# Order of ScalarE's work between attention and the GLU in a hybrid S5/attention block: the gates' sigmoids behind the last attention copies and v's second rounded half

## The chip, the cores and the metric

One core of a Trainium2 chip runs the whole block in one launch. The metric is the device time of an execution in microseconds (us); the kernel before takes 375.18 us, the median of three runs (375.08, 375.18 and 377.10).

## The reference

The block is a decoder layer over 256 tokens of width 1024. What matters here is its first half:

```
u = rms_norm(h, g_pre_mix)
z = u @ w_in                                  # [ssm | q | k | v | gate_A | gate_B]
y_a = v * sigmoid(v @ w_glu + b_glu)          # v = gelu(S5 output)
y_b = softmax(causal(q @ k.T / 8)) @ v_att    # 8 heads of 64
merged = sigmoid(z_ga) * (y_a @ w_branch_a) + sigmoid(z_gb) * (y_b @ w_branch_b)
h = h + rms_norm(merged @ w_out, g_post_mix)
f = square(relu(rms_norm(h, g_pre_ffn) @ w_ff1)) @ w_ff2
h = h + rms_norm(f, g_post_ffn)
```

All matrices are float32. With 256 tokens there is a single attention block, so the attention is causal over all of them.

## The kernel before, in words

**Weights in pieces.** The weights stream from HBM as pieces of 128x1024 float32 (512 KB), numbered in the order of use: 0 to 31 are `w_in` (ssm, k, q, v, then four chunks of gates, four pieces each; 28 to 31 are the last gates chunk), 32 and 33 `w_glu`, 34 to 37 `w_branch_b`, 38 to 41 `w_branch_a`, 42 to 49 `w_out`, then the MLP. SyncE's queue starts the loads, three raw buffers deep. Each piece is cut in two rounded parts: ScalarE (ACT in the profile) copies it to `w_hi` (L180), VectorE (DVE) subtracts to get `w_lo` (L181). Activations are cut in the same way (`v_h`, `v_l`; `yb_h`, `yb_l`; `ya_h`, `ya_l`). A product is then three matmuls, hi by hi, hi by lo and lo by hi (`three`, L204 to L206), and one piece is 24 matmuls of 256 columns (2 blocks of K, 4 of output, 3 products). There are five `w_hi`/`w_lo` buffers; `w_hi` of piece j waits until TensorE (PE) is done with piece j-5.

**Two K blocks per piece.** The GLU product v @ w_glu needs K blocks 0 and 1 with piece 32 and blocks 2 and 3 with piece 33; v's blocks 0 and 1 come from the first half of the S5 outputs (`outputs(0, v)`), blocks 2 and 3 from the second (`outputs(1, v)`, L1003). The first w_branch_b product likewise needs attention's first head group with piece 34 and the second group with piece 35.

**Attention.** For each of two head groups: scores (L1027), masked maximum (DVE, L1034), exp (ACT, L1041), normalising (DVE, L1048), transposes on PE (L1058, L1059 into two tiles; L1064 into a third), their copies to SBUF on ACT (`pT0`, two copies, L1060; `pT1`, L1065), then the products with the values (L1076) and the copy and subtraction to `yb_h` (ACT, L1079) and `yb_l` (DVE, L1080).

**ACT's function tables.** Exp, gelu and sigmoid each need a table load on ACT (ACT_TABLE_LOAD rows); plain copies (`AF.Copy`) run between them without one. A helper keeps functions of one table together by telling the scheduler what an instruction must come behind:

```
def table(name, inst, *before):
    for b in before:
        if b in last_act:
            follow(inst, last_act[b])
    last_act[name] = inst
```

`follow(later, earlier)` adds an order without a semaphore: a scheduler fixes the order of instructions on each engine when the program is built, from priorities and these orders, and on the chip each engine takes its instructions in that order. `sigmoid` (L437) serves the gates (`gate`: gate B in `sg_87`, gate A in `sg_86`, four sigmoids of 128x512 each) and the GLU (`sgl`, four of 128x256).

**Order around the change.** After the second gelu ACT has, in this order: a table load, seven gate sigmoids, the two `pT0` copies of the second group, `v_h`'s second half, the `pT1` copy, `w_hi` of piece 36, the eighth gate sigmoid, `w_hi` of piece 37, `yb_h`, and the GLU's sigmoids with `w_hi` of piece 38 among them. PE has the first half of the GLU, then the value products (L1076) with the GLU's second half around them, then w_branch_b.

Of the kernel before, what the change touches and what calls it, by code (L numbers as in the profile page):

```python
# [13 lines left out]
AF = mybir.ActivationFunctionType  # L14
# [4 lines left out]
P = 128  # L19
# [52 lines left out]
def pair_b(t):  # L72
    return t.unsqueeze(1).to_broadcast([P, 2, T])
# [3 lines left out]
def tile_hybrid_block(ctx, tc, a, out):  # L77


    nc = tc.nc  # L80
# [30 lines left out]
    def follow(later, earlier):  # L111

        tc.add_manual_dep(later.ins, earlier.ins.name, ORDER, reason="order")

    last_act, hold, marks, mains = {}, {}, {}, {}
# [7 lines that stand above are left out]
# [56 lines left out]
    def split(hi, lo, src):  # L179
        i = nc.scalar.activation(hi, src, AF.Copy)  # L180
        j = nc.vector.tensor_tensor(lo, src, hi.bitcast(F32), op=ALU.subtract)  # L181
        return i, j
# [174 lines left out]
    att = Attention(nc, att_pool, mask, ident, aux, table, soon)  # L357
# [68 lines left out]
    for g in range(2):  # L426
        for c in range(2):
            ps = chunk(KT, xh, xl)
            for j in range(2):
                s = sg[g][:, 4 * c + 2 * j:4 * c + 2 * j + 2, :]  # L430
                nc.vector.tensor_tensor(s, ps[j], pair_b(rs_b), op=ALU.mult)
    follow(s5.first_state[1], mains[28, 1])
    s5_pool.close()
    yb_h, yb_l = att.yb_h, att.yb_l

    def sigmoid(o, i, **kw):
        table("sigmoid", nc.scalar.activation(o, i, AF.Sigmoid, **kw), "gelu")  # L437

    def gate(g, c):
        for j in range(2):  # L440
            s = sg[g][:, 4 * c + 2 * j:4 * c + 2 * j + 2, :]
            sigmoid(s, s)
# [5 lines left out]
    v_h = mid.tile([P, 4, T], F32R, name="v_h")  # L448
    v_l = mid.tile([P, 4, T], F32R, name="v_l")
# [9 lines left out]
    vf = v.rearrange("p m b a -> p m (b a)")  # L459
    for j in range(2):  # L460
        js = slice(2 * j, 2 * j + 2)
        split(v_h[:, js, :], v_l[:, js, :], vf[:, js, :])

    def branch_b(c):
        pb = chunk(4, yb_h, yb_l)
# [5 lines left out]
    with ahead():  # L471
        for h in range(2):
            sgl = mid.tile([P, 2, T], F32, name="sgl", bufs=2)
            hs = slice(2 * h, 2 * h + 2)
            for e in range(2):
                sigmoid(sgl[:, e, :], ps[h][:, e, :], bias=b_glu[:, 2 * h + e:2 * h + e + 1])
            nc.vector.tensor_tensor(sgl, sgl, vf[:, hs, :], op=ALU.mult)
            for e in range(2):
                m = 2 * h + e
                split(ya_h[:, m, :].rearrange("p (a b) -> p b a", b=L), ya_l[:, m, :].rearrange("p (a b) -> p b a", b=L),  # L480
                      sgl[:, e, :].rearrange("p (b a) -> p b a", b=L))
# [69 lines left out]
    def turn(tt, kts, get=aux):  # L551

        tp = get((P, len(kts), P))
        for e, kt in enumerate(kts):
            i = nc.tensor.transpose(tp[:, e, :], h_tok[:, tt, P * kt:P * kt + P], ident)
        return tp, i
# [40 lines left out]
    for kts in (lower, upper):  # L597
        tp, _ = turn(1, kts)
# [6 lines left out]
    with at(SECOND):  # L605
        for tt in range(2):
            ss = small.tile([P, 2], F32, name="ss")
            for c in range(2):
                junk = small.tile([P, 512], F32, name="junk")
                i = nc.scalar.activation(junk, h_tok[:, tt, 512 * c:512 * c + 512], AF.Square, scale=1.0 / 32,  # L610
                                         accum_out=ss[:, c:c + 1])
# [73 lines left out]
class S5:  # L685
# [228 lines left out]
    def transposes(self):  # L914

        nc, B4 = self.nc, self.B4
        self.B4T = B4T = [t.rearrange("p i b c -> p i (b c)") for t in B4]
        for i4 in range(4):
            for j in range(2):
                tp = self.aux((P, 4, P))  # L920
                with self.soon() as side:
                    for i in range(4):
                        side(nc.tensor.transpose(tp[:, i, :], B4T[j][:, 4 * i4 + i, :], self.ident))
                nc.scalar.activation(B4T[j][:, 4 * i4:4 * i4 + 4, :], tp, AF.Copy)  # L924
# [81 lines left out]
class Attention:  # L1006
# [43 lines left out]
    def transposes(self):  # L1050

        nc, (p0, p1) = self.nc, self.prob
        for f in range(2):
            tp = self.aux((P, 2, T))
            with self.soon() as side:
                for e in range(2):
                    h = 2 * f + e
                    side(nc.tensor.transpose(tp[:, e, 0:P], p0[:, h, :], self.ident))  # L1058
                    side(nc.tensor.transpose(tp[:, e, P:T], p1[:, h, 0:P], self.ident))  # L1059
            nc.scalar.activation(self.pT0[:, 2 * f:2 * f + 2, :], tp, AF.Copy)  # L1060
        tp = self.aux((P, 4, P))
        with self.soon() as side:
            for h in range(4):
                side(nc.tensor.transpose(tp[:, h, :], p1[:, h, P:T], self.ident))  # L1064
        nc.scalar.activation(self.pT1, tp, AF.Copy)  # L1065

    def values(self, g, v_tok):
        nc = self.nc
# [88 lines left out]
```

## Time and profile before

| | us |
|---|---|
| median of 3 runs | 375.18 |
| the profiled execution, its own time | 375.54 |
| its span, first to last instruction | 373.7 |
| time outside the span (375.54 - 373.7) | 1.84 |
| PE busy in the span | 358.7 |
| DVE busy | 267.2 |
| ACT busy | 212.7 |

Times in the views below count from the start of the span. PE, DVE, ACT, POOL and SP are TensorE, VectorE, ScalarE, GpSimd and SyncE; L437 is line 437 of the kernel before. A row of the timeline gives start and duration, and in brackets the idle time before it with what ended that idle time. PEclk is the granted TensorE clock: 1.00 is 2.4 GHz and 0.50 is 1.2 GHz. Matmuls are pipelined, so their rows overlap and the distance between two starts is what one costs.

### The profile page before, as it was taken

What the parts mean: (1) busy time and instruction counts of PE and PEld (TensorE: products, weight loads), DVE (VectorE), ACT (ScalarE), POOL (GpSimd) and SP (SyncE); (2) the same over time, 40 slices, a digit from 0 to 9 for tenths busy, and PEclk for the clock granted to TensorE, in tenths of its full rate; (3) what the DMA queues carried; (4) which work ended last, traced back from release to release, by engine and by line L of the source; (5) the groups of instructions that cost most, each with busy time, mean ns of one, the idle gap of its engine ahead of it and who ended that gap; (6) DMA issues with size and microseconds to landing.
All of it is one profiled execution on the core that took longest, in us unless ns stands there. A gap on an engine that the chain in (4) does not pass through costs nothing.

```text
span 373.7 us, 7568 instructions
## 1 busy us (share of the span) xinstructions
PE 358.7 (96%) x3073; PEld 324.6 (87%) x3073; DVE 267.2 (71%) x459; ACT 212.7 (57%) x322; POOL 36.6 (10%) x46
## 2 busy tenths in 40 slices
PE   7999999999999869999999999999999999999993
PEld 6999979997998659998878989899898989989882
DVE  4999899999679826796768584655656475565633
ACT  4894539997963896454548653535345353533511
POOL 4005300001000000000001030202002020100200
PEclk9999999999999988999999999999999999999999
DMA  7966845465061525655634646665566656555303
GB/s 207 348 199 187 234 165 179 154 200 175 31 220 61 188 97 164 182 188 186 228 123 158 217 151 217 210 219 189 190 194 190 194 185 201 192 193 191 127 0 113
DMA packets 19604, 65.84 MB, mean 176 GB/s; under 512 B 2640, under 2 KB 3280, under 8 KB 19440
## 3 DMA queue, kind: packets, MB, share of 16 engines
q1 hardware_dynamic: 18624, 64.66, 53.4%
q0 software_dynamic: 512, 0.53, 0.6%
q8 instruction: 24, 0.39, 0.4%
q10 hardware_dynamic: 432, 0.17, 0.2%
q14 instruction: 12, 0.10, 0.1%
HBM read 63.77 MB, written 1.05 MB: 173 GB/s over the span
## 4 chain that ended last, share of the span: by engine, by line
PE 60%; ACT 12%; DVE 11%; DMA 10%; issue 4%; POOL 1%; SPq 0%; DVEq 0%; POOLq 0%; ACTq 0%
PE acc L211 10%; PE acc L210 10%; PE acc L209 10%; DMA w_raw<-in_w_in_dram 9%; PE aux L204 8%; PE aux L206 8%; PE aux L205 8%; DVE w_lo L181 4%; ACT w_hi L180 3%; ACT Tl L951 2%; PE acc L204 1%; PE acc L205 1%; PE acc L206 1%; DMA w_raw<-in_w_glu_dram 1%; ACT B L924 1%
## 5 line engine op out<-in xcount | busy, mean ns | idle before, releaser
L180 ACT ACTIVATE w_hi<-w_raw 128x1024 fp32r<-128x1024 f32 (+2 forms) x119 | 121.3, 1025 | 123.7 <-PE aux L205 37.4
L181 DVE TENSOR_TENSOR w_lo<-w_raw,w_hi 128x1024 fp32r<-128x1024 f32 (+2 forms) x119 | 139.7, 1177 | 70.7 <-ACT w_hi L180 70.3
L204 PE MATMUL acc<-xh,w_hi 128*128 128x256 f32 x224 | 63.2, 287 | 1.5 <-ACT w_hi L180 1.5
L205 PE MATMUL acc<-xl,w_hi 128*128 128x256 f32 x224 | 63.3, 286 | 0.0
L204 PE MATMUL aux<-h_h,w_hi 128*128 128x256 f32 x224 | 62.2, 278 | 0.0
L205 PE MATMUL aux<-h_l,w_hi 128*128 128x256 f32 x224 | 61.9, 276 | 0.0
L206 PE MATMUL aux<-h_h,w_lo 128*128 128x256 f32 x224 | 61.8, 276 | 0.0
L206 PE MATMUL acc<-xh,w_lo 128*128 128x256 f32 x224 | 60.5, 286 | 0.0
L210 PE MATMUL acc<-w_lo,f_h 128*128 128x512 f32 x128 | 50.0, 392 | 0.0
L211 PE MATMUL acc<-w_hi,f_l 128*128 128x512 f32 x128 | 49.9, 394 | 0.0
L209 PE MATMUL acc<-w_hi,f_h 128*128 128x512 f32 x128 | 49.5, 388 | 0.0
L204 PEld LDWEIGHTS acc<-xh,w_hi 128*128 128x128 f32 x224 | 43.1, 193 | 2.8 <-ACT w_hi L180 2.4
L205 PEld LDWEIGHTS acc<-xl,w_hi 128*128 128x128 f32 x224 | 43.4, 194 | 0.8 <-issue 0.7
L204 PEld LDWEIGHTS aux<-h_h,w_hi 128*128 128x128 f32 x224 | 42.1, 188 | 0.3
L205 PEld LDWEIGHTS aux<-h_l,w_hi 128*128 128x128 f32 x224 | 42.1, 188 | 0.3
L206 PEld LDWEIGHTS acc<-xh,w_lo 128*128 128x128 f32 x224 | 41.5, 192 | 0.9 <-issue 0.5
L206 PEld LDWEIGHTS aux<-h_h,w_lo 128*128 128x128 f32 x224 | 42.0, 188 | 0.0
L69 POOL TENSOR_TENSOR r<-r 128x512 f32<-128x512 f32 x14 | 17.8, 1289 | 128.7 <-ACT f_h L647 128.7
L210 PEld LDWEIGHTS acc<-w_lo,f_h 128*128 128x128 f32 x128 | 24.0, 188 | 5.3
L209 PEld LDWEIGHTS acc<-w_hi,f_h 128*128 128x128 f32 x128 | 24.0, 188 | 5.1
L211 PEld LDWEIGHTS acc<-w_hi,f_l 128*128 128x128 f32 x128 | 24.1, 188 | 4.8
L649 DVE TENSOR_TENSOR f_l<-r,f_h 128x512 fp32r<-128x512 f32 x14 | 15.3, 1095 | 6.5 <-POOL r L69 6.5
(245 smaller groups left out, 564.6 us busy)
## 6 DMA issues: line engine op xcount, KB each, us to landing
w_raw<-in_w_ff_dram SPq DMA_DIRECT2D x64, 512.0 KB, 4.8
w_raw<-in_w_in_dram SPq DMA_DIRECT2D x31, 512.0 KB, 4.2
w_raw<-in_w_out_dram SPq DMA_DIRECT2D x8, 512.0 KB, 4.7
w_raw<-in_w_bb_dram SPq DMA_DIRECT2D x4, 512.0 KB, 4.8
w_raw<-in_w_ba_dram SPq DMA_DIRECT2D x4, 512.0 KB, 4.0
w_raw<-in_w_glu_dram SPq DMA_DIRECT2D x2, 512.0 KB, 4.4
x_tok<-in_xt_dram SPq DMA_DIRECT2D x1, 1024.0 KB, 8.0
g_row<-in_rows_dram SPq DMA_DIRECT2D x2, 512.0 KB, 6.1
```

What stands on the lines that cost most here:

```text
L69: return nc.gpsimd.tensor_tensor(o, x, y, op=op)
L180: i = nc.scalar.activation(hi, src, AF.Copy)
L181: j = nc.vector.tensor_tensor(lo, src, hi.bitcast(F32), op=ALU.subtract)
L204: first = nc.tensor.matmul(o, lhsT=wh, rhs=xh, start=start, stop=False)
L205: nc.tensor.matmul(o, lhsT=wh, rhs=xl, start=False, stop=False)
L206: return first, nc.tensor.matmul(o, lhsT=wl, rhs=xh, start=False, stop=stop)
L209: first = nc.tensor.matmul(o, lhsT=xh, rhs=wh, start=start, stop=False)
L210: nc.tensor.matmul(o, lhsT=xh, rhs=wl, start=False, stop=False)
L211: nc.tensor.matmul(o, lhsT=xl, rhs=wh, start=False, stop=stop)
L649: nc.vector.tensor_sub(f_l[:, js, :], r, f_h[:, js, :].bitcast(F32))
L924: nc.scalar.activation(B4T[j][:, 4 * i4:4 * i4 + 4, :], tp, AF.Copy)
L951: nc.scalar.activation(o, i, AF.Copy)
```

## The change

Three orders are added. Sigmoids must come behind the last copy into `pT1` and behind `v_h`'s second half (before, behind the second gelu alone). To have something to point to, `v_h`'s copies and the `pT1` copy are noted in `last_act`. And the first transpose of attention's second group must come behind the matmuls of the first K block of piece 31, the last gates piece.

```diff
@@ -430,11 +430,12 @@
     follow(s5.first_state[1], mains[28, 1])
+    follow(att.turned[0], mains[31, 0])
     s5_pool.close()
...
     def sigmoid(o, i, **kw):
-        table("sigmoid", nc.scalar.activation(o, i, AF.Sigmoid, **kw), "gelu")
+        table("sigmoid", nc.scalar.activation(o, i, AF.Sigmoid, **kw), "gelu", "v_h", "pT")
...
@@ -459,7 +460,7 @@
     for j in range(2):
         js = slice(2 * j, 2 * j + 2)
-        split(v_h[:, js, :], v_l[:, js, :], vf[:, js, :])
+        last_act["v_h"], _ = split(v_h[:, js, :], v_l[:, js, :], vf[:, js, :])
...
@@ -1050,19 +1051,20 @@
     def transposes(self):
 
         nc, (p0, p1) = self.nc, self.prob
+        self.turned = []
...
                     h = 2 * f + e
-                    side(nc.tensor.transpose(tp[:, e, 0:P], p0[:, h, :], self.ident))
+                    self.turned.append(side(nc.tensor.transpose(tp[:, e, 0:P], p0[:, h, :], self.ident)))
...
-        nc.scalar.activation(self.pT1, tp, AF.Copy)
+        self.table("pT", nc.scalar.activation(self.pT1, tp, AF.Copy))
```

What the scheduler makes of it on ACT, from the second gelu on (`sg_87` is gate B, `sg_86` gate A, `pT_366` is pT0, `pT_367` is pT1). Before:

```order
L1003 ACT_TABLE_LOAD
L1003 ACTIVATE v<-aux 128x512
L437 ACT_TABLE_LOAD
L437 ACTIVATE sg_87<-sg_87 128x512 x3
L437 ACTIVATE sg_86<-sg_86 128x512 x4
L1060 ACTIVATE pT_366<-aux 128x512 x2
L180 ACTIVATE v_h<-v 128x512
L1065 ACTIVATE pT_367<-aux 128x512
L180 ACTIVATE w_hi<-w_raw 128x1024
L437 ACTIVATE sg_87<-sg_87 128x512
L180 ACTIVATE w_hi<-w_raw 128x1024
L1079 ACTIVATE yb_h<-aux 128x512
```

and with the change (lines behind the inserted ones are one or two higher):

```order
L1004 ACT_TABLE_LOAD
L1004 ACTIVATE v<-aux 128x512
L1062 ACTIVATE pT_366<-aux 128x512 x2
L180 ACTIVATE v_h<-v 128x512
L1067 ACTIVATE pT_367<-aux 128x512
L438 ACT_TABLE_LOAD
L438 ACTIVATE sg_87<-sg_87 128x512 x3
L180 ACTIVATE w_hi<-w_raw 128x1024
L438 ACTIVATE sg_86<-sg_86 128x512 x4
L438 ACTIVATE sg_87<-sg_87 128x512
L180 ACTIVATE w_hi<-w_raw 128x1024
L1081 ACTIVATE yb_h<-aux 128x512
```

The second table load and the seven sigmoids have gone from ahead of the four copies to behind them, piece 36's `w_hi` (the first of the two) now stands among the sigmoids, and between the gelu and `yb_h` stand the same instructions as before. Further down, `w_hi` of piece 39 stands ahead of all four `ya_h` copies where it stood between the second and the third, and on DVE the subtractions for `ya_l`, piece 39's `w_lo` and the first gate products (L468) change places with each other.

On PE, at the end of the GLU's first half (`v_h`, `v_l` with piece 32), before:

```order
L205 MATMUL acc<-v_l,w_hi 128x256
L206 MATMUL acc<-v_h,w_lo 128x256
L204 MATMUL acc<-v_h,w_hi 128x256
L205 MATMUL acc<-v_l,w_hi 128x256
L206 MATMUL acc<-v_h,w_lo 128x256
L1076 MATMUL aux<-pT_366,v_tok 64x256 x2
L204 MATMUL acc<-v_h,w_hi 128x256 x2
L1076 MATMUL aux<-pT_367,v_tok 64x128 x2
```

and with the change:

```order
L205 MATMUL acc<-v_l,w_hi 128x256
L1078 MATMUL aux<-pT_366,v_tok 64x256 x2
L206 MATMUL acc<-v_h,w_lo 128x256
L204 MATMUL acc<-v_h,w_hi 128x256
L205 MATMUL acc<-v_l,w_hi 128x256
L206 MATMUL acc<-v_h,w_lo 128x256
L204 MATMUL acc<-v_h,w_hi 128x256 x2
L1078 MATMUL aux<-pT_367,v_tok 64x128 x2
```

The first two value products have moved ahead of the last four matmuls of piece 32; no other row of PE has moved, the transposes of the second group among them.

## Rows read from the trace of the kernel before

**Rows 1.** The page: PE's busy time, and its granted clock in 40 slices.
```profile
PE 358.7 (96%) x3073; PEld 324.6 (87%) x3073; DVE 267.2 (71%) x459; ACT 212.7 (57%) x322; POOL 36.6 (10%) x46
...
PEclk9999999999999988999999999999999999999999
```

**Rows 2.** The chain that ended last, 118 to 170 us: start, us, what.
```profile
132.78 2.69 ACT sg L437 x5
...
137.01 0.79 PE acc L204 x2
```

**Rows 3.** Timeline of ACT, second gelu to the GLU's first sigmoid.
```profile
129.81 0.60 ACT L1003 ACTIVATE v<-aux 128x512 f32<-128x512 f32 x1
130.43 1.28 ACT L437 ACT_TABLE_LOAD   x1
131.72 3.75 ACT L437 ACTIVATE sg<-sg 128x512 f32<-128x512 f32 x7
135.38 1.06 ACT L1060 ACTIVATE pT<-aux 128x512 f32<-128x512 f32 x2
136.33 0.62 ACT L180 ACTIVATE v_h<-v 128x512 fp32r<-128x512 f32 x1
136.85 0.59 ACT L1065 ACTIVATE pT<-aux 128x512 f32<-128x512 f32 x1
137.33 1.06 ACT L180 ACTIVATE w_hi<-w_raw 128x1024 fp32r<-128x1024 f32 x1
...
139.75 0.60 ACT L1079 ACTIVATE yb_h<-aux 128x512 fp32r<-128x512 f32 x1
143.46 0.84 ACT L437 ACTIVATE sgl<-acc,cols 128x256 f32<-128x256 f32 x2 [3.11 <-PE acc L206]
```

**Rows 4.** Timeline of PE, second group's transposes to w_branch_b's second half.
```profile
128.64 0.33 PE L1059 MATMUL aux<-shp,prob 128*128 128x128 f32 x1 [1.19 <-DVE prob L1048]
...
129.60 0.60 PE L1064 MATMUL aux<-shp,prob 128*128 128x128 f32 x4
...
132.66 0.28 PE L206 MATMUL acc<-v_h,w_lo 128*128 128x256 f32 x1
...
133.00 0.28 PE L206 MATMUL acc<-v_h,w_lo 128*128 128x256 f32 x1
136.01 0.65 PE L1076 MATMUL aux<-pT,v_tok 128*64 128x256 f32 x4 [2.73 <-ACT pT L1060]
...
139.64 0.58 PE L205 MATMUL acc<-v_l,w_hi 128*128 128x256 f32 x1
...
144.04 0.28 PE L204 MATMUL acc<-yb_h,w_hi 128*128 128x256 f32 x1
...
146.76 0.39 PE L204 MATMUL acc<-yb_h,w_hi 128*128 128x256 f32 x2
146.98 0.28 PE L205 MATMUL acc<-yb_l,w_hi 128*128 128x256 f32 x1
```

**Rows 5.** Timeline of PE, the last value products of the first head group.
```profile
116.17 1.09 PE L1076 MATMUL aux<-pT,v_tok 128*64 128x128 f32 x12
```

**Rows 6.** Timeline of DVE: w_lo of piece 37, yb_l, the last ya_l.
```profile
139.88 1.23 DVE L181 TENSOR_TENSOR w_lo<-w_raw,w_hi 128x1024 fp32r<-128x1024 f32 x1 [0.24 <-ACT w_hi L180]
141.03 0.68 DVE L1080 TENSOR_TENSOR yb_l<-aux,yb_h 128x512 fp32r<-128x512 f32 x1
...
149.25 1.19 DVE L181 TENSOR_TENSOR ya_l<-sgl,ya_h 128x256 fp32r<-128x256 f32 x2
```

**Rows 7.** Windows: stretch, busy PE PEld DVE ACT POOL, PEclk, DMA share, GB/s.
```profile
136.50:137.00 0.50, 0.16 (x2) 0.00 (x0) 0.01 (x1) 0.50 (x2) 0.00 (x0) 0.62 0.00 0
...
143.00:143.50 0.50, 0.50 (x4) 0.50 (x4) 0.00 (x0) 0.04 (x1) 0.00 (x0) 0.56 0.94 352
```

**Rows 8.** PE's waits after 137 us: us in total, times, longest.
```profile
PE acc L211 <- DVE h_l L566: 0.4, 1, 0.4
```

**Rows 9.** The page's DMA issues: count, KB each, median us to landing.
```profile
w_raw<-in_w_ba_dram SPq DMA_DIRECT2D x4, 512.0 KB, 4.0
```

## The prediction

> **What bounds the kernel now.** The page says that PE is busy for 96% of the span [rows 1], so PE is the engine to free. Two slices of 40 have a lower granted clock, the fifteenth and sixteenth (131 to 149 us), and the change lies there. The chain of waits then tells who holds PE: it runs through five of the gate sigmoids on ACT and comes back to PE at 137.01, in the GLU's second half [rows 2]. The timeline of ACT shows why. The second gelu ends at about 130.41; then come 1.28 us of table load and seven sigmoids (131.72 to 135.38, 0.523 each), and only then the two pT0 copies, v_h and pT1, for which PE is waiting [rows 3]. PE has issued the last matmul of piece 32 at 133.00, stands idle for 2.73 us until the first pT0 copy, and gets v_h just before 137.01 [rows 4]. The clock goes from 1.00 to 0.50 inside 136.50 to 137.00, after that stand, and is back to 1.00 inside 143.00 to 143.50 [rows 7], so nearly all the second half of the GLU runs at 1.2 GHz: its last 22 matmuls take 4.40 us (139.64 to 144.04 [rows 4]), 0.20 each, where three matmuls before the stand took 0.34 us (132.66 to 133.00), 0.113 each. From 144.04 PE waits for others for 0.4 us in all the rest of the kernel [rows 8]: what moves 144.04 moves the end.
>
> **The change, step by step.** I follow ACT first, then DVE, then PE, with the times of the profiled execution. No instruction is added or taken away and the table loads are as many as before, so only the places count.
>
> ACT. From the gelu to yb_h it does the same ten groups of work, without an idle moment in the trace before [rows 3]. In the new order the copies take the front: pT0 twice from 130.43 to 131.38 (135.38 to 136.33 before, 0.95), v_h to 131.90 (0.52), pT1 to 132.38 (0.48). Their inputs are there: the transposes into the two pT0 tiles are out before 129.60, where the last four (for pT1) begin, 0.60 long [rows 4]. Each copy is **4.95 us earlier**. The table load then runs to 133.66, three sigmoids to 135.23, w_hi of piece 36 to 136.18 (0.95, 2.1 us earlier than before, cost nothing), five sigmoids to 138.80, w_hi of piece 37 to 139.75, and yb_h starts at 139.75 as before: a sum of the same terms in another order. It ends at about 140.35.
>
> DVE. w_lo of piece 37 comes behind its w_hi, so at 139.88 as before, and yb_l behind that, 141.03 to 141.71 [rows 6]. **That is what is late next**: yb_l of the second head group does not get earlier at all.
>
> PE. The first two value products now stand at 132.66 and find their pT0 copy done (131.0); I price them at 0.65, the row before, at full clock [rows 4]. To 133.31. The four last matmuls of piece 32 then take 0.45, and I allow 0.1 for the change of shape: 133.86. v_h and v_l of the second half are there (131.90, and a subtraction later on DVE), so two matmuls follow, to 134.09, with no stand of 2.73 us. The rest of the value products, twelve records, cost 1.09 at full clock in the first group [rows 5], and pT1 is long there: 135.18. The 22 remaining GLU matmuls at 0.113 take 2.49: **the GLU ends at 137.7 instead of 144.04**. The first half of w_branch_b (piece 34, K blocks of the first head group, split long ago) needs nothing new and takes 2.72 as before (144.04 to 146.76): 140.4. There the second half starts. Its two first matmuls need yb_h, done at 140.35; the third needs yb_l, done at 141.71. So PE stands again, for about 1.1 us beside those two matmuls, and that matmul starts at about 141.76 where it started at 146.98 [rows 4]. **Gain 5.22 us.**
>
> The other way round: the 2.73 of idle time goes, so does the 0.35 between the value products (136.01 and 0.65 of length) and 137.01, and the stretch from 137.01 to 144.04, 7.03 at 1.2 GHz, becomes 3.84 at 2.4 GHz (133.86 to 137.7), 3.19 less. That is 6.27, and 1.1 of new idle time comes: 5.2 again. The one number that decides is yb_l's end, and it rests on ACT's and DVE's rows, not on PE's: PE may lose a whole microsecond on its way before anything changes.
>
> Behind that, PE must stay fed. The GLU's sigmoids need the GLU's result (137.7) and ACT after yb_h, so they start at about 140.4 instead of 143.46 [rows 3], 3.1 earlier, while PE is 5.2 earlier: their lead shrinks by 2.1. Before, the last ya_l ended at 150.44 [rows 6], and w_branch_a, which starts 96 matmuls after 144.04, at 154.9, wants it with its second piece at 157.6: a lead of 7.2, now some 5. The loads keep pace: piece 39's is started by w_lo of piece 36, 2.1 earlier. I take nothing for this part. The third edit, the order for the first transpose, moves no row on PE: nothing.
>
> Edges. A gain beyond 5.2 would need yb_l earlier; if it were not waited for at all, 6.3 (368.9). Below, if PE's own path is a microsecond longer than I have it, the stand just shrinks; two longer cost one (4.2, 371.0).
>
> The profiled execution took 375.54, 0.36 above the median of the three runs. From its span the sum gives 375.54 - 5.22 = 370.3; from the median, 370.0, and that is my number.
>
> **The rivals.**
>
> *The clock falls again.* The new stands of PE, about 1.1 us at 140.6 to 141.7, follow 9 us of dense work. In the trace a stand of 1.19 us at 127.45 to 128.64 [rows 4] left the clock full, in the slice before the two low ones [rows 1], and one of 2.73 did not [rows 7]; 1.1 is nearest to the first. If it falls all the same, and for as long as before (136.6 to 143.4, 6.8 us), PE loses half of that, 3.4: 373.4, or 371.7 if it is back after half the time. The Trainium skill, "TensorE: Matmul & The Clock Gate", section "A second HAM failure mode: psum-queue depth-cycling", says that frequent short idle times between groups of matmuls make the clock go down and up; by that rule this rival would be the likely one and the time 371.7 to 373.4, while the stand of 1.19 us in this trace speaks against it. Chance 0.09.
>
> *Part is given back later.* The lead of ya_h and ya_l, or of w_lo of pieces 40 and 41, is shorter than I count it and PE stands at w_branch_a for 1 to 2 us: 371 to 372. For it: ACT's end does not move up (yb_h at 139.75), and four ya_h now stand behind w_hi of piece 39. Against it: leads of 5 us. Chance 0.07.
>
> *The bound is ACT, not PE.* The rest would follow yb_h, which does not move, and nothing is gained: 375.2, within 0.5%. Against it: 3.11 us of ACT idle right behind yb_h [rows 3], and PE's next 210 us almost without a wait [rows 8]. Chance 0.04.
>
> *Slower.* The one instruction that can do this is w_hi of piece 39, now ahead of all four ya_h on ACT, which takes its instructions in order: if its load is late, ya_h is late, then PE at w_branch_a. That load starts at about 137.5 and takes 4.0 by the median [rows 9], against about 143 when ACT comes to it. It costs from a landing at about 147 on, and the kernel is slower than before only from about 152, some 15 us after its start; at 153.5 the time would be 370.0 + 6.5 = 376.5. Nothing in the page has such a landing. Chance 0.03.
>
> **How the numbers follow.** The forecast, 370.0, has 0.77, with its own range 369.2 to 371.0. I reach to 372.2, which takes in the second rival and half of the first, and down to 368.9, the edge without the wait for yb_l; left out are the long clock fall, no gain and slower, and half a chance in ten for a miss of the terms: some 0.18. A measurement of this kernel can tell about 0.5%, 1.9 us, from no change. Faster by more than that (below 373.3) are the forecast, the second rival and most of the first: 0.91. Within 0.5%: the ACT rival and the longest clock fall, 0.06. Slower: 0.03.
>
> **What would show it.** On ACT the pT0 copies directly behind the gelu, the sigmoid table load about 2 us later, and yb_h within 0.3 us of where it was. On PE no wait for pT0 or v_h; the value products at a clock of 1.00, and PEclk full in slices fifteen and sixteen; the only new wait one of about 1.1 us for yb_l, in w_branch_b; then PE rows 5.2 us earlier to the end. The step is wrong if PE's new wait is longer than 2 us, if the clock drops anywhere between 131 and 160, or if PE waits at w_branch_a.

## The result and the profile after

The changed kernel takes 371.86 us, the median of four runs (371.20 to 372.06), against 375.24 for the kernel before; the ratio is 0.990, with a 95% interval of 0.986 to 0.993, a gain of 2.7 to 5.2 us. The profiled execution took 372.06, its span is 370.3, and its mean clock is 0.998 where that of the kernel before was 0.989.

The page of the changed kernel has no slice below 9 in the clock any more, where two stood [rows 1]:

```profile
PE 355.8 (96%) x3073; PEld 320.5 (87%) x3073; DVE 266.8 (72%) x459; ACT 212.3 (57%) x322; POOL 36.7 (10%) x46
...
PEclk9999999999999999999999999999999999999999
```

The timeline of ACT after the change answers to [rows 3]. The copies for PE come right behind the gelu, the table load 2.1 us later, and yb_h is where it was: 9.98 us behind the gelu's start (140.57 - 130.59), before 9.94 (139.75 - 129.81).

```profile
130.59 0.60 ACT L1004 ACTIVATE v<-aux 128x512 f32<-128x512 f32 x1
131.09 1.08 ACT L1062 ACTIVATE pT<-aux 128x512 f32<-128x512 f32 x2
132.04 0.64 ACT L180 ACTIVATE v_h<-v 128x512 fp32r<-128x512 f32 x1
132.56 0.61 ACT L1067 ACTIVATE pT<-aux 128x512 f32<-128x512 f32 x1
133.19 1.28 ACT L438 ACT_TABLE_LOAD   x1
134.49 1.67 ACT L438 ACTIVATE sg<-sg 128x512 f32<-128x512 f32 x3
136.06 1.04 ACT L180 ACTIVATE w_hi<-w_raw 128x1024 fp32r<-128x1024 f32 x1
137.01 2.70 ACT L438 ACTIVATE sg<-sg 128x512 f32<-128x512 f32 x5
139.62 1.04 ACT L180 ACTIVATE w_hi<-w_raw 128x1024 fp32r<-128x1024 f32 x1
140.57 0.57 ACT L1081 ACTIVATE yb_h<-aux 128x512 fp32r<-128x512 f32 x1
```

The timeline of PE answers to [rows 4]. The value products (L1078) and the GLU's second half run through without the stand of 2.73 us, w_branch_b starts at 138.63, and PE then waits for yb_l alone:

```profile
133.52 0.65 PE L1078 MATMUL aux<-pT,v_tok 128*64 128x256 f32 x4
...
135.00 1.09 PE L1078 MATMUL aux<-pT,v_tok 128*64 128x128 f32 x12
...
138.63 0.28 PE L204 MATMUL acc<-yb_h,w_hi 128*128 128x256 f32 x1
...
142.57 0.38 PE L205 MATMUL acc<-yb_l,w_hi 128*128 128x256 f32 x1 [0.83 <-DVE yb_l L1082]
...
182.67 1.29 PE L556 MATMUL aux<-shp,h_tok 128*128 128x128 f32 x8 [0.39 <-DVE h_tok L515]
```

The wait in the last of these rows is new too. The row is the first transposes of h_tok, behind the first half of the post-mix norm; before, they ran without a wait.

Executions differ in how long they take up to the second gelu, so the stretches behind it are compared by their distance from the gelu's start. The table has all kernels of this study, from their timelines; e1 to e8 are the experiments of the next section. w_branch_a is the first matmul from ya_h. h_tok is the result of the first half of the post-mix norm, and its column has the first of its transposes on PE. The end is that of the span.

| kernel | gelu starts | to w_branch_a | to h_tok | to the end | clock in the GLU and w_branch_b |
|---|---|---|---|---|---|
| before | 129.81 | 25.11 | 56.59 | 243.89 | falls |
| changed | 130.59 | 20.04 | 52.08 | 239.71 | full |
| e1 (same order) | 128.79 | 20.05 | 51.73 | 239.31 | full |
| e8 (the same again) | 129.81 | 20.04 | 52.25 | 239.79 | full |
| e2 before, filled | 129.59 | 22.19 | 53.68 | 241.01 | full |
| e3 squares first | 128.74 | 20.03 | 51.52 | 238.96 | full |
| e4 yb first | 131.05 | 18.92 | 52.67 | 240.25 | full |
| e5 both | 128.75 | 18.92 | 50.50 | 238.35 | full |
| e6 behind v_h only | 130.53 | 26.34 | 58.65 | 246.07 | falls |
| e7 lo40 first | 130.70 | 20.03 | 51.79 | 239.40 | full |

So the 3.48 us between the two profiled executions (375.54 and 372.06) are 5.07 gained up to w_branch_a, 0.56 given back by h_tok, 0.33 more by the end (4.18 left), and 0.78 that the second execution was late at the gelu, ahead of everything that the change moves. These sum to 3.40; the rest lies outside the span.

### The profile page after: what moved, and what is told of

Read it like the earlier page. It is cut to its first block, busy times and chain, and to the rows that moved or that the text cites. A ratio compares the mean times of both kernels' runs of the same rounds, so it can differ in the third digit from the quotient of the medians.

```text
span 370.3 us, 7568 instructions
## 1 busy us (share of the span) xinstructions
PE 355.8 (96%) x3073; PEld 320.5 (87%) x3073; DVE 266.8 (72%) x459; ACT 212.3 (57%) x322; POOL 36.7 (10%) x46
## 4 chain that ended last, share of the span: by engine, by line
PE 67%; DVE 14%; DMA 8%; ACT 6%; issue 3%; SPq 0%; POOL 0%; DVEq 0%; POOLq 0%; ACTq 0%
PE acc L211 9%; PE acc L210 9%; PE acc L209 9%; PE aux L205 7%; PE aux L204 7%; PE aux L206 7%; DVE w_lo L181 5%; DMA w_raw<-in_w_in_dram 5%; PE acc L206 4%; PE acc L205 4%; PE acc L204 4%; ACT w_hi L180 2%; DMA w_raw<-in_w_out_dram 2%; DMA w_raw<-in_w_ff_dram 1%; PE aux L964 1%
## 5 line engine op out<-in xcount | busy, mean ns | idle before, releaser
L205 PE MATMUL acc<-xl,w_hi 128*128 128x256 f32 x224 | 62.4, 283 | 0.0
L205 PEld LDWEIGHTS acc<-xl,w_hi 128*128 128x128 f32 x224 | 42.6, 190 | 0.9 <-issue 0.7
```

Of the source, the lines that this page charges most:

```text
L205: nc.tensor.matmul(o, lhsT=wh, rhs=xl, start=False, stop=False)
```

## The experiments

e1 to e4 were measured on one chip, where the kernel before has a median of 375.57 us, and e5 to e8 on another, where it has 374.43. Times are therefore compared within a group or by their ratio to the kernel before.

**The order without the third edit, and the changed kernel again.** e1 leaves out the order for the first transpose; e8 is the changed kernel word for word.

```diff
-    follow(att.turned[0], mains[31, 0])
```

> The changed kernel without its third edit (the order for the first transpose). Theory A (the 1.8 us that are missing against the forecast of 370.0 come from two places: about 0.8 that the profiled execution had lost before the second gelu, by the way its first loads landed, and 0.8 to 0.9 given back at the transposes of h_tok, L556): the third edit moves no instruction, so this is the changed kernel once more, 371.2 to 372.1, its profile again shows a wait for yb_l of 0.8 us in w_branch_b and the stand at L556, and the time of the second gelu differs from 130.6 by some tenths of a us, either way. Theory B (the third edit counts on the chip): another time, over 0.5 us away from 371.9.

> The changed kernel once more, word for word, on the same chip as the three above, for their comparison. Expected from the two profiles of this order so far: w_branch_a 20.0 us after the second gelu, h_tok's transposes 51.7 to 52.1 after it, time 371.3 to 372.1, and a start of the execution (up to the gelu) that differs from run to run by up to 1 us either way. If instead the late start of the first profile (gelu at 130.59 against 129.81 before) comes with the change, the gelu is at 130.4 or later again.

e1 took 371.35 (ratio to the kernel before 0.990, 0.987 to 0.993) and e8 371.13 (0.991, 0.988 to 0.994). In the table both repeat the changed kernel to 0.1 us up to w_branch_a. The order of instructions is the same with and without the third edit on every engine, so it does nothing, as forecast. The gelu starts at 128.79 and 129.81: the late start of the first profile is not the change's. Over the ten executions of the table, whose order is the same up to there, it lies between 128.74 and 131.05. h_tok's transposes vary more than w_branch_a: the profiles of the changed kernel, e1 and e8, all of this order, have 52.08, 51.73 and 52.25, with waits of 0.39, none and 0.56; theory A had expected the wait in e1 too.

**The clock alone.** e2 leaves ACT's order as it was before and puts 20 matmuls that nothing reads into PE's stand.

```diff
+            if g:
+                one = self.ident.bitcast(BF16)
+                self.fill = [side(nc.tensor.matmul(yp[:, 0, :], lhsT=one[:, 0:P], rhs=one, start=True, stop=True))
+                             for _ in range(20)]
...
     ps = chunk(4, v_h, v_l)
+    follow(att.fill[0], mains[32, 1])
```

> The kernel before, with 20 matmuls of 256 bf16 columns that nothing reads put on PE behind the GLU's first half, where it stands for 2.73 us; they write the tile of the value products, which those then start anew. No order on ACT changes. Theory A (the idle time cost 3.1 us and the low clock behind it another 3.2 us): the fill takes 2.2 us, the clock stays at 1.00, the 22 last GLU matmuls take 2.5 us instead of 4.4, w_branch_b starts at about 140.9 instead of 144.04 and the time is 372.1 to 372.6, some 2.7 to 3.1 us below the kernel before. Theory B (the clock falls for another reason, or its fall costs nothing because yb_l or the loads end last): 375.2 and the GLU's second half at half clock or w_branch_b at 144.

e2 took 372.73 (ratio 0.996, 0.994 to 0.998), 0.1 above the range of theory A. PE's timeline in e2, and one of its windows behind the fill (columns as in [rows 7]):

```profile
132.88 2.36 PE L1074 MATMUL aux<-shp 128*128 128x256 bf16 x20
135.78 0.65 PE L1081 MATMUL aux<-pT,v_tok 128*64 128x256 f32 x4 [0.54 <-ACT pT L1061]
137.27 1.09 PE L1081 MATMUL aux<-pT,v_tok 128*64 128x128 f32 x12
140.90 0.28 PE L204 MATMUL acc<-yb_h,w_hi 128*128 128x256 f32 x1
...
139.00:139.50 0.50, 0.50 (x7) 0.50 (x6) 0.42 (x1) 0.50 (x1) 0.00 (x0) 1.00 0.00 0
```

The clock stays full, the twelve value records take 1.09 as in the first group [rows 5], and w_branch_b starts at 140.90, as expected. Against the gelu that is 2.92 us earlier than before (11.31 instead of 14.23), with ACT's order and its copies where they were. More than half of the 5.07 us was clock, not waiting: matmuls without any use, in time that was idle anyway, win that part back.

**What gives back 0.2 to 0.7 us by h_tok.** That is by how much less than 5.07 us h_tok's transposes have gained in e1 (0.20), the changed kernel (0.56) and e8 (0.73). In the timeline of ACT of the changed kernel the norm's squares (L509) stand behind w_hi of piece 52, which waits for its load. On DVE the norm's first step (gm, L505) stands behind w_lo of the same piece:

```profile
175.26 1.06 ACT L180 ACTIVATE w_hi<-w_raw 128x1024 fp32r<-128x1024 f32 x1 [1.12 <-DMA w_raw<-in_w_ff_dram]
178.04 1.06 ACT L180 ACTIVATE w_hi<-w_raw 128x1024 fp32r<-128x1024 f32 x1 [1.73 <-DMA w_raw<-in_w_ff_dram]
179.01 0.58 ACT L509 ACTIVATE junk<-acc 128x512 f32<-128x512 f32 x1
...
179.14 1.23 DVE L181 TENSOR_TENSOR w_lo<-w_raw,w_hi 128x1024 fp32r<-128x1024 f32 x1 [1.56 <-ACT w_hi L180]
180.28 0.69 DVE L505 TENSOR_TENSOR gm<-acc,g_row 128x512 f32<-128x512 f32 x1
```

The chain that ended last runs through DVE: the load, w_hi and w_lo of piece 52, gm, the rest of the norm, h_tok. The squares are done by then. In the kernel before, both stood there too, but PE was later:

```profile
181.45 1.06 ACT L180 ACTIVATE w_hi<-w_raw 128x1024 fp32r<-128x1024 f32 x1 [1.30 <-DMA w_raw<-in_w_ff_dram]
182.41 0.58 ACT L508 ACTIVATE junk<-acc 128x512 f32<-128x512 f32 x1
```

Against the gelu the squares moved up by 4.18 us (52.60 to 48.42), PE by 5.07. The table follows this place through the runs that leave the norm behind piece 52. "Step" is the distance on PE from the start of the last matmul to the first transpose of h_tok; it shows a delay that the bracket misses where the idle time is short.

| kernel | w_hi of piece 52, behind the gelu | h_tok behind that w_hi | step on PE |
|---|---|---|---|
| before | 51.64 | 4.95 | 0.23 |
| e2 | 48.88 | 4.80 | 0.24 |
| e6 | 53.68 | 4.97 | 0.23 |
| changed | 47.45 | 4.63 | 0.79 |
| e1 | 47.10 | 4.63 | 0.43 |
| e8 | 47.62 | 4.63 | 0.96 |
| e7 | 47.17 | 4.62 | 0.51 |
| e4 | 48.05 | 4.62 | 2.49 |

Where PE is late (before, e2, e6) its step is 0.23 or 0.24 and nothing is lost there. In the other five h_tok comes 4.62 or 4.63 us behind w_hi of piece 52, whenever that starts, and the step exceeds 0.23 by what is given back. e3 puts the squares, and the norm's first half on DVE, ahead of piece 52; `splits` and `lows` hold the two roundings of each piece.

```diff
...
+    sq, last = norm_out(pm[0], 0, g_row, gm, h_tok, x_tok)
+    follow(splits[52], sq)
+    follow(lows[52], last)
```

> The changed kernel with the first two squares of the post-mix norm (L509) ahead of w_hi of piece 52 on ACT, and the norm's last step for the first token half ahead of w_lo of piece 52 on DVE. Theory A (the norm stands behind the rounding of a piece whose load has become late against PE, which costs 0.8 us at L556): no stand of PE at L556, 0.6 to 0.9 us faster than the changed kernel, 371.0 to 371.3. Theory B (the 0.9 us come from somewhere else, or the pieces 52 and 53, now rounded later, are late in their turn): no gain, 371.8 or more, with a wait of PE for w_hi or w_lo in the first MLP group.

e3 took 370.45 (ratio 0.990, 0.986 to 0.993; e1 in the same comparison 371.35), below the range of theory A. ACT in e3:

```profile
174.06 0.58 ACT L509 ACTIVATE junk<-acc 128x512 f32<-128x512 f32 x1
...
176.34 0.60 ACT L509 ACTIVATE junk<-acc 128x512 f32<-128x512 f32 x1 [1.60 <-PE acc L211]
176.92 2.00 ACT L180 ACTIVATE w_hi<-w_raw 128x1024 fp32r<-128x1024 f32 x2
```

Now the second square waits for PE's sum, and no step of the norm waits for a load. h_tok comes 51.52 behind the gelu, 5.07 earlier than before: **all of the gain arrives there**, and 4.93 of it at the end. Theory A holds; the gain over e1 by the medians, 0.9 us, is within the scatter, and the row of the table is what decides. The 0.1 to 0.3 us that this and the changed order lose between h_tok and the end were not traced.

**PE's path shortened further.** e4 puts yb_h's copy ahead of the sigmoids as well.

```diff
-        table("sigmoid", nc.scalar.activation(o, i, AF.Sigmoid, **kw), "gelu", "v_h", "pT")
+        table("sigmoid", nc.scalar.activation(o, i, AF.Sigmoid, **kw), "gelu", "v_h", "pT", "yb")
...
-        nc.scalar.activation(self.yb_h[:, gs, :], yp, AF.Copy)
+        self.table("yb", nc.scalar.activation(self.yb_h[:, gs, :], yp, AF.Copy))
```

> The changed kernel with the sigmoids also behind yb_h's copy, so that yb_h and yb_l come before the sigmoid table is loaded. Theory A (in w_branch_b PE waits for yb_l alone, and behind it the loads and DVE set the pace): no wait of PE in w_branch_b (0.83 us in the changed kernel), w_branch_b 0.8 us earlier against the gelu, but less of it left at the end: 371.0 to 371.7. Theory B (PE is the only bound behind w_branch_b): all 0.8 us are left at the end, 371.0 or less. Theory C (the GLU's sigmoids, now 1 us later, hold up ya_h and w_branch_a): 372 or more with a wait of PE for ya_h or ya_l.

e4 took 372.66 (ratio 0.993, 0.991 to 0.996). That is above the 371.35 of e1, though the two intervals overlap; in the table its end is 0.5 to 0.9 later than those of the changed order. None of the three theories had that time with its cause. The wait for yb_l is gone and w_branch_a is another 1.1 us earlier (18.92), but PE's waits have a new first place behind the gelu:

```profile
PE aux L556 <- DVE h_tok L515: 2.1, 1, 2.1
```

and ACT shows the same cause, larger:

```profile
179.10 1.06 ACT L180 ACTIVATE w_hi<-w_raw 128x1024 fp32r<-128x1024 f32 x1 [2.03 <-DMA w_raw<-in_w_ff_dram]
180.07 0.58 ACT L509 ACTIVATE junk<-acc 128x512 f32<-128x512 f32 x1
```

Theory A had the direction, not the size: 2.27 us of 6.19 are lost at this one step (2.49 instead of 0.23). Against the changed kernel, PE is 1.12 earlier and w_hi of piece 52 is 0.60 later, since its load is later too (43.12 behind the gelu instead of 42.45); these two make up the further loss of 1.71. e5 has both edits:

> The two edits together: sigmoids also behind yb_h's copy, and the first two squares and the first half of the post-mix norm ahead of the rounding of piece 52. Theory A (PE's path is 6.2 us shorter than before up to w_branch_a, and what yb_first gave back was lost at L556 alone, behind the rounding of piece 52): from the second gelu to the transposes of h_tok about 50.5 us (before 56.6, changed kernel 52.1, yb_first alone 52.7), no stand at L556, time 2.2 to 2.5 us below yb_first alone and about 1 us below squares_first alone, near 369.5 to 370.3. Theory B (the loads themselves are late, not only what stands behind them on ACT): PE waits in the first MLP group for pieces 50 to 53 instead, and the time is within 0.5 us of squares_first alone.

e5 took 369.30 (ratio 0.987, 0.983 to 0.990), the lowest ratio of all, with h_tok at 50.50 as expected and the time 0.2 below the range. It is faster than both kernels: 1.83 below e8, the changed kernel on the same chip.

**The sigmoids behind v_h alone.** e6 drops the order behind pT1, and ACT's order changes: pT1 then comes behind seven sigmoids, yb_h behind the GLU's.

```diff
-        table("sigmoid", nc.scalar.activation(o, i, AF.Sigmoid, **kw), "gelu", "v_h", "pT")
+        table("sigmoid", nc.scalar.activation(o, i, AF.Sigmoid, **kw), "gelu", "v_h")
```

> The changed kernel with the sigmoids behind v_h's second half, but no longer behind the pT1 copy: ACT then takes six sigmoids, w_hi of piece 36 and one more sigmoid ahead of pT1, and the GLU's sigmoids with two more w_hi ahead of yb_h. Theory A (what decides is yb_l): the GLU is not held up, but yb_l ends at about 14.4 us after the second gelu's start instead of 11.9, PE stands for about 3.5 us in w_branch_b, and w_branch_a starts 22.5 us after the gelu if the clock stays at 1.00 (changed kernel 20.0, before 25.1), up to 25.7 if the clock falls for as long as it did before; time 373.5 to 376. Theory B (v_h's place is all that counts): as the changed kernel, 371 to 372, w_branch_a at 20.

e6 took 378.03 (ratio 1.009, 1.006 to 1.013): **slower than before**. PE's waits in e6 behind the gelu:

```profile
PE acc L204 <- ACT yb_h L1081: 3.6, 1, 3.6
...
PE acc L205 <- DVE yb_l L1082: 0.6, 1, 0.6
```

and the clock in its windows (columns as in [rows 7]):

```profile
144.00:144.50 0.50, 0.00 (x0) 0.00 (x0) 0.18 (x1) 0.50 (x2) 0.00 (x0) 0.82 0.60 180
144.50:145.00 0.50, 0.00 (x0) 0.00 (x0) 0.48 (x1) 0.50 (x2) 0.00 (x0) 0.50 0.91 319
...
151.00:151.50 0.50, 0.50 (x6) 0.50 (x5) 0.09 (x1) 0.22 (x1) 0.00 (x0) 0.86 0.00 0
```

The stand was sized right (3.6 against 3.5) and the clock fell for some 7 us, but w_branch_a came at 26.34 where 25.7 was expected at the most, and the time lies 2 us above the range. The forecast had yb_l at 14.4 us; PE got it at 15.87 (146.40 - 130.53), 1.5 later. Two things were left out: ahead of yb_h, ACT waits 0.45 us for the load of piece 39, and on DVE yb_l stands behind w_lo of that piece (144.52, 1.23 us). Behind the low clock, too, PE was slower than priced: up to the end of w_branch_a its matmuls of 256 columns start 0.118 us apart, where the other profiles have 0.113, with the granted clock at 1.00 in both. From w_branch_a to h_tok PE takes 0.83 us longer than before (32.31 against 31.48); the cause is not shown. That the second half of yb is what decides holds, yb_h with 3.6 us and yb_l with 0.6; theory B falls.

**Where the loads begin to lag.** A load can start when the raw buffer of the piece three before it is free, that is when DVE has done that piece's w_lo. e7 frees piece 40's raw buffer earlier on DVE: the four ya_l subtractions (`yas`) come behind its w_lo.

```diff
...
+        if c == 1:
+            for i in yas:
+                follow(i, lows[40])
```

> The changed kernel with the four ya_l subtractions behind w_lo of piece 40 on DVE, so that this raw buffer comes free some 2 us earlier and the load of piece 43 starts earlier. Theory A (the lag of the loads begins at DVE, which works without a break from w_lo of piece 37 on): loads 43 and later start 1 to 2 us earlier against the gelu, the squares at L509 come earlier and the stand at L556 is gone or half as long; 0.3 to 0.8 us faster than the changed kernel. Theory B (the lag arises again at each later piece, from three raw buffers and some 4.5 us per load, whatever happens at piece 40): loads 46 and later start when they did, L556 as in the changed kernel, no gain.

e7 took 370.31 (ratio 0.990, 0.987 to 0.993). The starts of some loads, in us behind the gelu:

| load of piece | 39 | 40 | 43 | 46 | 47 | 51 | 52 |
|---|---|---|---|---|---|---|---|
| before | 9.86 | 11.33 | 22.97 | 30.26 | 33.80 | 44.76 | 46.82 |
| changed | 7.80 | 11.36 | 19.94 | 26.40 | 29.94 | 39.70 | 42.45 |
| e8 (the same again) | 7.80 | 11.35 | 19.94 | 26.57 | 30.10 | 40.74 | 42.62 |
| e7 | 7.80 | 11.35 | 18.01 | 25.76 | 29.30 | 40.51 | 41.79 |

Between before and changed, the load of piece 39 is 2.06 earlier, that of piece 40 not at all, those of pieces 43, 47 and 52 3.0, 3.9 and 4.4, all short of PE's 5.07. Piece 40 waits for w_lo of piece 37, which starts 10.07 behind the gelu before and 10.10 after and takes 1.23: w_hi of that piece stands just ahead of yb_h and moved no more than yb_h did.

Of the 1.9 us that e7 gains at piece 43 against e8, 0.8 are left at pieces 46, 47 and 52 and 0.2 at piece 51: less than theory A has, more than theory B. h_tok comes at 51.79 (52.25 in e8), but e1 has 51.73 without this edit. The run doesn't tell its theories apart.

## Why the prediction was right, and where it was off

**The direction, the mechanism and the price at its place were right.** The sum had PE's third matmul of w_branch_b's second half 5.22 us earlier; it is 11.98 us behind the gelu's start (142.57 - 130.59) where it was 17.17, so 5.19. Each step is in the rows: the copies behind the gelu, yb_h unmoved, the value products at 0.65 and 1.09, w_branch_b 8.04 behind the gelu against 7.9 forecast, a new wait of 0.83 against 1.1. e2 confirms the split into clock and waiting: the clock was priced at 3.19 us, and e2 gains 2.92 by it alone.

**The time was met only by the wide range, in part by luck.** 371.86 lies outside 369.2 to 371.0, which had the chance of 0.77, and inside the stretch up to 372.2, which was added for a give-back at w_branch_a and a short fall of the clock. Neither happened; in the profiled execution other things filled that stretch: 0.56 us of lost lead by h_tok, 0.33 behind it that were not traced, and 0.78 of a late start.

**The step that failed is "The loads keep pace" and "I take nothing for this part", on what feeds PE behind w_branch_b.** I looked at ya_l and found a lead of 5 us, which held: PE never waited at w_branch_a. I looked at the load of piece 39 alone, and not at that of piece 40, which doesn't move at all. And I left out that the norm's steps stand on ACT and DVE behind a piece that waits for its load. Of the w_hi of pieces 41 to 52, eight waited for PE to free a buffer before and three for a DMA; after, it is three and seven. The second rival had the mechanism, give-back through lost lead, with a chance of 0.07, but at the wrong place; by the three profiles 0.2 to 0.7 us are gone at h_tok, and 4.10 to 4.58 us of 5.07 are left at the end. e3 and e5 show the place, e4 the direction: more lead lost, more given back.

**The other term was not in the sum at all:** the start of the execution. The forecast took the profiled execution to be within 0.36 us of the median, and executions differ by 2.3 us at the gelu alone. By the medians the gain is 3.4 us here, and 4.2 and 3.3 in the two later comparisons (e1 and e8), so the times alone fix it to about 1 us; the distances from the gelu are what shows the parts.

**The rivals.** The clock did not fall at the new stand of 0.83 us: it stayed at 1.00 through stands of 1.19 and 0.83 us, and in e4 through one of 2.10, while it went to 0.50 (1.2 GHz) just behind the stand of 2.73 us before [rows 7] and inside that of 3.59 us in e6. The Trainium skill, "TensorE: Matmul & The Clock Gate", section "A second HAM failure mode: psum-queue depth-cycling", was cited for a fall at frequent short idle times between groups of matmuls; the single short stands of these traces, 0.83 to 2.10 us, didn't show one. ACT as the bound is refuted by the result: yb_h did not move, and the end came 4.18 us earlier. The slower rival did not occur, yet slower was one order away: e6 has it by yb_h and the clock, and w_hi of piece 39 has a part of 0.45 us in it, by its wait ahead of yb_h.

## What to carry to other kernels

When a stall of the busiest engine goes, ask for every stage behind it how much lead its inputs had and what keeps their pace; the gain arrives only as far as the shortest lead reaches, and a step that waits in an in-order queue behind an unrelated piece is where it shows. Price a stall of PE with the low clock that can follow it: here the clock was over half of the gain on PE's path, and unused matmuls in the gap won that part back without touching the order of anything else. And measure from a landmark ahead of the change, since the start of an execution can scatter by more than the effect.

## What the runs showed that I had not expected

Twenty bf16 matmuls whose result nothing reads, 2.36 us of PE time in a gap, made a kernel 2.9 us shorter behind the gelu (e2). And the time up to the second gelu scattered by 2.3 us between executions of the same order of instructions; in the two profiles of before and after, the rounding of the fourth weight piece started at 14.68 and 15.75 us, so the difference is there while the first loads land, for which both roundings wait. Why they land differently was not tried. PE's pace differs between executions too: from 58 to 70 us matmuls of 256 columns start 0.118 us apart in the kernel before and 0.113 in the changed one, at the same granted clock of 1.00. What part of the scatter this is, and why it is so, is open.
